# Running the long convolution among the steps of the recurrence, with each of its products split into two of 64 columns

## The chip, the cores and the metric

The kernel is one program on one core of a Trainium2 chip. The metric is device microseconds (us) of one execution, smaller is better. The kernel before takes 4325.55 us (median of 3 runs, 4324.6 to 4327.83).

## The reference

The model has two blocks. The part that matters here lies in its second block, in a layer whose input is projected, in one dense product, to the inputs of two branches. One branch is a recurrence over tokens, the other a long convolution; a dense output layer takes both results.

```python
def wkv_scan(s0, r, decay, k, v, kk, b, reverse, emit):
    def step(s, inp):
        r_t, w_t, k_t, v_t, kk_t, b_t = inp
        sa = jnp.einsum('bhij,bhj->bhi', s, kk_t)
        s = s * w_t[:, :, None, :] - sa[..., None] * b_t[:, :, None, :] + v_t[..., None] * k_t[:, :, None, :]
        y = jnp.einsum('bhij,bhj->bhi', s, r_t) if emit else None
        return s, y
    ...

def fft_long_conv(z, kern, skip):
    L = z.shape[1]
    zf = jnp.fft.rfft(z.astype(jnp.float32), n=2 * L, axis=1)
    kf = jnp.fft.rfft(kern, n=2 * L, axis=0)
    y = jnp.fft.irfft(zf * kf[None], n=2 * L, axis=1)[:, :L]
    return (y + z * skip).astype(z.dtype)

def hyena_operator(u, short_taps, kern, skip):
    v, x1, x2 = split_cols(centred_conv3(u, short_taps), (HY_WIDTH, HY_WIDTH, HY_WIDTH))
    z = v
    for o, gate in enumerate((x1, x2)):
        z = gate * fft_long_conv(z, kern[:, o], skip[o])
    return z
```

The recurrence runs for 8 heads of 64 channels and in two directions, first over 256 context tokens, then over 1024 latent tokens, where it also emits y. A readout normalises the sum of both directions' y for each head. The convolution is of order 2 over 512 channels and 1024 tokens.

## The kernel before, in words

Inside this layer the work comes in four stages, one after another.

1. **The dense input layer** (`rec_dense`). Its tasks are interleaved with the preparation of features (`rwkv_features`), among them `rwkv_inverse(who)`, which inverts small triangular matrices by doubling, with a product (L1660) and a subtraction (L1662) per step, and stores tables to DRAM (`d_T`). In this stage it runs for the head pairs 0 and 1 and for the context (`None`).
2. **The convolution** (`hyena`). `yH` holds the 512 channels as four tiles `ct` of 128 x 1024 tokens. For each order o and each half hh of 256 channels the tokens are transposed into `z` (L1268), go through a forward transform (L1281: a 128 x 128 block of the table `F` is stationary, 256 columns of z move), are combined and multiplied with the spectrum `K` on DVE (all through the helper `add`, L1271), giving `G`, and go back (L1338: a 128 x 128 block of G is stationary, 256 columns of the table `I` move). DVE then updates `yH`. The inverse products of one half are issued between the forward ones of the next.
3. **The recurrence** (`rwkv_chains`, `rwkv_scan`). Tokens are taken in 20 chunks of 64, heads in four pairs. A *chain* is one pair in one direction. Four chains run at once: pairs 0 and 1 in both directions for 20 steps, then pairs 2 and 3 for 20 more, 40 steps in all. Every four steps a chain has one load (`load`: be, LK, T and SV by DMA from SP's queue) and one preparation (`prep`: p2 at L1741, masked on DVE at L1746; pt at L1753, copied to `tm` by ACT at L1755; two more products L1763 and L1771, copied into AE and T). `LK` and `T` alternate between two buffers. A step (`steps`) has four parts, with a `yield` between them: pr (L1789) and its copy R; pu (L1799) and its copy `uv`, half on ACT and half on DVE; ps (L1806) and the new state (L1809, DVE: ps * PL + sp, where sp = SV * PL was made on POOL at L1795); py (L1815), copied or added into `yB`. The inverses of the pairs 2 and 3 run between the steps of the first 20 (`later`), on POOL, and the readouts of pairs 0 and 1 between the last 20 (`slow`).
4. **The dense output layer**, beside which the readouts of pairs 2 and 3 run.

A scheduler orders the instructions of each engine from the order in which the generators issue them and from when buffers come free, so each engine's order is near the code's, and not equal to it. The eight PSUM banks are shared out by name (`self.banks(name=count)`); a bank is taken anew when the last instruction that reads it is done. Bank and tile names in the orders below end in numbers that tell one use from another.

## Time and profile before

| what | us |
|---|---|
| median of 3 runs | 4325.55 |
| profiled execution | 4318.2 |
| its span | 4316.1 |
| end of the dense input layer | 1855 |
| convolution | 1855 to 2054 |
| recurrence | 2054 to 2454 |
| dense output layer | 2454 to 2546 |

The table's times come from the profiled execution, whose mean granted clock of PE is 0.939. The bounds of the stages are read from the instructions at their edges. In the profile, engines are PE (matrix products), PEld (its weight loads), DVE, ACT and POOL (elementwise) and SP (which issues most DMAs). A row of the groups gives line, engine, operation, result and operands with their shapes, count, then busy time, mean ns of one, then the idle time of the engine just ahead of them and what ended it. A row of the timeline gives start, length, engine, line, operation and how many instructions it stands for. A float32 product leaves two records.

### The profile page before, as it was taken

The page shows a single profiled execution, that of the slowest core. Times are in us where ns is not written, and L with a number is a line of the kernel's source. Part 1 is how long each engine was busy: PE and PEld are TensorE (multiplying, and loading weights), DVE is VectorE, ACT ScalarE, POOL GpSimd, SP SyncE. Part 2 cuts the span into 40 slices and gives each one's busy share as a digit, 9 for nine tenths or more (in the row PEclk, how much of TensorE's full clock was granted, in tenths as well). Part 3 has the DMA queues.
Part 4 walks back from the last instruction along what each step waited for, and adds up shares of the span by engine and source line. Part 5 has one row for each costly group of instructions (what it writes and reads, how often), then busy time and mean ns, then how long its engine had stood idle before and what let it go on. Part 6 is the DMA issues. An engine that isn't in the chain of part 4 may idle for free.

```text
span 4316.1 us, 65300 instructions
## 1 busy us (share of the span) xinstructions
PE 3887.0 (90%) x23789; PEld 3168.0 (73%) x23789; DVE 2779.1 (64%) x5935; ACT 1781.4 (41%) x3746; POOL 1357.6 (31%) x1570
## 2 busy tenths in 40 slices
PE   7989998899999988977686888999997897999999
PEld 4768886777787767766675766777876785888787
DVE  7842426788844767759565656599777768656532
ACT  6433415777735544411453423334336523333311
POOL 5422302333324432300564334122212116554200
PEclk8899998999999999988897999999998998999999
DMA  5444326421234544531543323233336351222422
GB/s 209 151 168 164 130 75 168 122 70 31 78 109 127 184 143 135 170 144 67 134 124 107 111 65 115 93 105 116 122 105 172 105 185 58 88 79 83 151 102 74
DMA packets 351338, 511.29 MB, mean 118 GB/s; under 512 B 149864, under 2 KB 226424, under 8 KB 348329
## 3 DMA queue, kind: packets, MB, share of 16 engines
q1 hardware_dynamic: 332200, 436.33, 32.1%
q0 software_dynamic: 14064, 53.48, 3.6%
q10 hardware_dynamic: 4752, 17.30, 1.3%
q8 instruction: 188, 3.08, 0.3%
q14 instruction: 134, 1.09, 0.1%
HBM read 343.69 MB, written 164.63 MB: 118 GB/s over the span
## 4 chain that ended last, share of the span: by engine, by line
PE 37%; DVE 7%; DMA 2%; ACT 2%; issue 1%; POOL 1%; SPq 1%; ACTq 0%; DVEq 0%; POOLq 0%
PE bank L285 18%; PE bank L2493 10%; PE bank L2393 2%; DMA SV<-d_V 1%; PE bank L1741 1%; PE bank L1789 1%; PE bank L724 1%; PE bank L1815 1%; PE bank L1753 1%; PE bank L685 1%; PE bank L246 0%; DVE d L2225 0%; DVE S L694 0%; DVE SV L1809 0%; DVE junk L2225 0%
## 5 line engine op out<-in xcount | busy, mean ns | idle before, releaser
L285 PE MATMUL bank<-hhi,whi 128*128 128x512 f32 (+1 forms) x1264 | 488.6, 387 | 13.1 <-ACT hhi L399 10.1
L285 PE MATMUL bank<-hlo,whi 128*128 128x512 f32 (+1 forms) x1264 | 485.0, 384 | 4.3 <-DVE hlo L400 2.1
L285 PE MATMUL bank<-hhi,wlo 128*128 128x512 f32 (+1 forms) x1264 | 482.6, 382 | 0.0
L267 ACT ACTIVATE whi<-wf 128x1024 fp32r<-128x1024 f32 (+3 forms) x202 | 193.5, 960 | 462.1 <-PE bank L285 393.0
L268 POOL TENSOR_TENSOR wlo<-wf,whi 128x1024 fp32r<-128x1024 f32 (+1 forms) x96 | 220.5, 2298 | 462.9 <-ACT whi L267 427.8
L285 PEld LDWEIGHTS bank<-hhi,whi 128*128 128x128 f32 x1264 | 243.8, 193 | 62.7 <-ACT hhi L399 10.9
L285 PEld LDWEIGHTS bank<-hlo,whi 128*128 128x128 f32 x1264 | 243.7, 193 | 54.5 <-DVE hlo L400 4.6
L285 PEld LDWEIGHTS bank<-hhi,wlo 128*128 128x128 f32 x1264 | 242.9, 192 | 46.7
L2493 PE MATMUL bank<-th,wh 128*128 128x512 f32 x616 | 247.3, 402 | 6.8 <-ACT th L2418 6.8
L2493 PE MATMUL bank<-th,wl 128*128 128x512 f32 x616 | 246.6, 400 | 0.0
L411 POOL CAST phi<-split 128x512 fp32r<-128x512 f32 (+1 forms) x104 | 62.7, 603 | 476.4 <-ACT split L410 381.0
L322 POOL TENSOR_TENSOR walo<-wa,wahi 128x512 fp32r<-128x512 f32 x96 | 137.0, 1441 | 238.4 <-ACT wahi L321 224.0
L285 PE MATMUL bank<-yT,whi 128*128 128x512 f32 (+1 forms) x600 | 190.6, 387 | 1.1 <-ACT ush L1393 0.5
L407 DVE TENSOR_TENSOR plo<-bank,phi 128x512 fp32r<-128x512 f32 (+2 forms) x260 | 166.5, 653 | 34.9 <-ACT phi L406 32.6
L406 ACT ACTIVATE phi<-bank 128x512 fp32r<-128x512 f32 (+2 forms) x260 | 143.5, 563 | 66.7 <-PE bank L724 25.4
L1795 POOL TENSOR_SCALAR sp<-SV,PL 64x64 f32<-64x64 f32 x304 | 135.9, 448 | 80.9 <-DVE SV L1809 59.4
L285 PE MATMUL bank<-yH,whi 128*128 128x512 f32 x376 | 151.4, 403 | 7.9 <-ACT ev_a L2156 4.4
L285 PE MATMUL bank<-yB,whi 128*128 128x512 f32 x376 | 150.6, 401 | 8.0 <-DVE yB L397 7.2
L285 PE MATMUL bank<-yH,wlo 128*128 128x512 f32 x376 | 150.4, 400 | 0.0
L268 DVE TENSOR_TENSOR wlo<-wf,whi 128x1024 fp32r<-128x1024 f32 (+2 forms) x106 | 117.6, 1112 | 50.8 <-ACT whi L267 50.6
L2493 PE MATMUL bank<-tl,wh 128*128 128x512 f32 x352 | 141.8, 403 | 6.4 <-DVE tl L2419 5.2
L2493 PEld LDWEIGHTS bank<-th,wh 128*128 128x128 f32 x616 | 117.7, 191 | 36.7 <-ACT th L2418 8.7
(632 smaller groups left out, 11275.9 us busy)
## 6 DMA issues: line engine op xcount, KB each, us to landing
wf<-in_w_in_dram SPq DMA_DIRECT2D x47, 512.0 KB, 3.5
wf<-in_w_ffn_in_dram SPq DMA_DIRECT2D x44, 512.0 KB, 3.4
d_rec<-r_rec SPq DMA_DIRECT2D x40, 512.0 KB, 3.6
wf<-in_rec_w_in_dram ACTq DMA_DIRECT2D x33, 512.0 KB, 3.9
wf<-in_attn_w_in_dram SPq DMA_DIRECT2D x26, 512.0 KB, 4.3
wa<-in_attn_ada_w_dram POOLq DMA_DIRECT2D x24, 512.0 KB, 4.0
wa<-in_rec_ada_w_dram POOLq DMA_DIRECT2D x24, 512.0 KB, 4.2
LK<-d_rec SPq DMA_DIRECT2D x64, 192.0 KB, 3.3
```

Of the source, the lines that this page charges most:

```text
L267: nc.scalar.activation(hi, wf, AF.Copy)
L268: self.wlo.tensor_tensor(lo, wf, hi, OP.subtract)
L285: self.mark = nc.tensor.matmul(ps[:, :n], w[:, k - k0, :], x(k, t0, n), start=(k == ks[0] and j == 0), stop=(k == ks[-1] and j == 2))
L322: nc.gpsimd.tensor_tensor(lo[:, k], w3[:, k], hi[:, k], OP.subtract)
L406: nc.scalar.activation(hi, src, AF.Copy)
L407: nc.vector.tensor_tensor(lo, src, hi, OP.subtract)
L411: nc.gpsimd.tensor_copy(hi, full)
L685: nc.tensor.matmul(bank[:, at:at + n], qs, kk[:, t0:t0 + n], start=(i == 0), stop=(i == 1))
L724: nc.tensor.matmul(o[:, c0:c0 + w], u["v"][:, kt, h, :], x[:, at:at + w], start=(kt == order[0] and j == 0), stop=(fin and j == 1))
L1795: nc.gpsimd.tensor_scalar(sp[half[h]], sv[half[h], h], pl[half[h]], None, OP.mult)
L2393: nc.tensor.matmul(ps, w[:, k, :], x[:, k, t0:t0 + n], start=(k == k0 and j == 0), stop=(k == k1 - 1 and j == 2))
L2493: self.mark = nc.tensor.matmul(ps, w[i][:, k, :], x[i][k], start=(k == 0 and j == 0), stop=(k == kh - 1 and j == 2))
```

## The change

The convolution becomes a generator (`hyena`) that runs between the steps of the recurrence (`scan_and_hyena`). It works by tiles of 128 channels, in eight rounds (o, ct), with halves of the buffers, and **every product is issued as two**, each with 64 stationary columns and 64 of the bank's partitions (`for h in (0, 64)`). Transposes become products with the identity. F and I are loaded at the start of the stage.

The recurrence runs **two chains at once instead of four**: both directions of one pair, one pair after another, 80 steps. Its banks are q=3 (pr, pu, ps), y=1, pt=1 for preparations, and X=2 for the convolution; readouts and inverses share one more. In a step, both halves of `uv` are copied by ACT; sp on POOL and the sum on DVE are gone: a product with the identity (L1792 of the kernel after) adds the state into the bank of ps, and ACT copies the bank into the next state with PL as scale. The second direction's y is copied by ACT and added on POOL. `uv`'s other half is loaded from DRAM where ACT copied it. A preparation has one bank in turn for its four products, and its masks come as two operations instead of four.

The inverse of pair 2 moves into the dense input layer; that of pair 3 runs between the first 20 steps. The readouts of pairs 0, 1 and 2 run between the steps of the next pair, and that of pair 3 beside the output layer.

```diff
-    def hyena(self, d_hy, d_sgh, yH):
...
-        self.banks(s=4, o=2, pt=2)
...
+    def hyena(self, pf, p, d_hy, d_sgh, yH):
...
+        for r in range(4):
+            nc.gpsimd.dma_start(yH[:, r], d_hy[r * 128:(r + 1) * 128, :])
+            self.load_r(F[:, r], A["dft_f1"][r])
+        for r in range(4):
+            self.load_r(I[:, r], A["dft_i1"][r])
+        yield
+        for o in range(2):
+            for ct in range(4):
+                G = []
+                yield from self.hyena_fwd(p, o, ct, F, yH, G)
+                yield from self.hyena_inv(p, o, ct, I, yH, G, d_hy, d_sgh)
...
-                    nc.tensor.transpose(ps[:, i * 128:(i + 1) * 128], zr[:, j // 2, (j % 2) * 128:(j % 2) * 128 + 128], self.ident)
...
+                for h in (0, 64):
+                    at = j % 2 * 128 + h
+                    nc.tensor.matmul(ps[h:h + 64, i * 128:(i + 1) * 128], zr[:, j // 2, at:at + 64], self.ident, start=True, stop=True)
...
-                        self.mark = nc.tensor.matmul(X[r][:, c], F[:, r, at:at + 128], z[:, r * 2 + k], start=(k == 0), stop=(k == 1))
+                        for h in (0, 64):
+                            at = k * 512 + c * 256 + f * 128 + h
+                            nc.tensor.matmul(X[r][h:h + 64, c], F[:, r, at:at + 64], z[:, r * 2 + k], start=(k == 0), stop=(k == 1))
...
-                            nc.tensor.matmul(ps[:, i, :], Gs[f][:, r, half, cc * 128:(cc + 1) * 128],
-                                             I[:, r, kt * 256:(kt + 1) * 256], start=(n == 0), stop=(n == 3))
+                        for h in (0, 64):
+                            nc.tensor.matmul(ps[h:h + 64, i, :], Gs[f][:, r, half, h:h + 64], I[:, r, kt * 256:(kt + 1) * 256],
+                                             start=(n == 0), stop=(n == 3))
...
+                                  (2, ("s", 3, 3), [("s", 2, g) for g in range(4)] + [("i", None)])):
...
-            later = [self.rwkv_inverse(p, pair, R, 1) for pair in (2, 3)]
-            self.banks(s=5, pt=2, o=1)
...
+            self.banks(q=3, y=1, X=2, pt=1, s=1)
+            self.share["o"] = self.share["s"]
+            self.rwkv_scan(p, R, yB, self.rwkv_inverse(p, 3, R, 1), self.hyena(q, q, R["hy"], R["sg"], yH))
...
+            for v in (x["S"], x["U"]):
+                for h in range(2):
+                    i = pair * 128 + h * 64
+                    nc.sync.dma_start(v[half[1 - h], :, h], R["V"][sg * 256:(sg + 1) * 256, i:i + 64].rearrange("(c s) i -> s c i", s=64))
...
-            p2 = [self.bank("pt", (128, 2, w, 64)) for _ in range(2)]
...
+            p2 = self.bank("pt", (128, 4, w, 64))
...
-                sp = T("sp", 4, 64)
-                for h in range(2):
-                    nc.gpsimd.tensor_scalar(sp[half[h]], sv[half[h], h], pl[half[h]], None, OP.mult)
...
-            nc.scalar.activation(uv[half[0], 0], pu[half[0]], AF.Copy)
-            nc.vector.tensor_copy(uv[half[1], 1], pu[half[1]])
...
+            for h in range(2):
+                nc.scalar.activation(uv[half[h], h], pu[half[h]], AF.Copy)
             if step < 19:
...
+                    nc.tensor.matmul(ps[half[h]], self.ident[:, half[h]], sv[:, h], start=True, stop=False)
+            yield
+            if step < 19:
+                for h in range(2):
+                    nc.tensor.matmul(ps[half[h]], tm[:, half[h]], uv[:, h], start=False, stop=True)
...
-                    nc.vector.scalar_tensor_tensor(s1[half[h], h], ps[half[h]], pl[half[h]], sp[half[h]], OP.mult, OP.add)
+                    nc.scalar.activation(s1[half[h], h], ps[half[h]], AF.Copy, scale=pl[half[h]])
...
+        for g in range(80):
...
+            gens = [steps(d, g) for d in range(2)]
...
             while gens or (preps and g % 4 == 3):
                 gens = [x for x in gens if next(x, 0) is None]
                 n += 1
+                turns += 1
                 if preps and g % 4 and next(preps[0], 0) is not None:
                     preps.pop(0)
...
+                if g < 20 and turns % 2:
+                    next(later, None)
+                if slow and n % 2 and next(slow[0], 0) is not None:
                     slow.pop(0)
+                if turns % 2:
+                    next(beside, None)
+        for _ in beside:
+            pass
```

The rows below are from the built orders of the two kernels: line, operation, result, operands, shape, and x with the number of like instructions in a row. Here is PE in the kernel before, in the middle of the convolution, where its transposes (L1268), inverse products (L1338) and forward products (L1281) stand.

```order
L1268 MATMUL bank4_4466_18930<-ident_1_66,yH_4394_18614 128x128 x4
L1268 MATMUL bank5_4469_18944<-ident_1_66,yH_4394_18614 128x128 x4
L1338 MATMUL bank6_4468_18939<-I_4404_18630,G_4453_18879 128x256 x2
L1338 MATMUL bank7_4471_18961<-I_4404_18630,G_4453_18879 128x256 x2
L1268 MATMUL bank4_4470_18954<-ident_1_66,yH_4394_18614 128x128 x4
L1268 MATMUL bank5_4472_18966<-ident_1_66,yH_4394_18614 128x128 x4
L1281 MATMUL bank0_4474_18978<-z_4465_18929,F_4395_18621 128x256 x4
```

And here is PE in the kernel after, in the convolution's second round: the forward products are now L1273, and the others belong to the recurrence (pr L1780, pu L1786, the identity L1792, ps L1796, py L1805) and to its preparations (L1763 and L1736, in bank6).

```order
L1273 MATMUL bank4_4619_20079<-z_4600_19958,F_4418_18767 64x128 x13
L1763 MATMUL bank6_4497_19330<-T11_4408_18734,AE1_4411_18740 64x32 x8
L1780 MATMUL bank1_4507_19379<-SV11_4445_18977,LK11_4407_18733 64x64 x2
L1786 MATMUL bank2_4511_19394<-R_4506_19377,T01_4403_18724 64x64 x2
L1792 MATMUL bank0_4512_19399<-SV01_4442_18965,ident_1_66 64x64 x2
L1273 MATMUL bank4_4619_20079<-z_4600_19958,F_4418_18767 64x128 x3
L1273 MATMUL bank5_4636_20166<-z_4600_19958,F_4418_18767 64x128 x11
L1786 MATMUL bank1_4513_19402<-R_4508_19382,T11_4408_18734 64x64 x2
L1792 MATMUL bank2_4514_19407<-SV11_4445_18977,ident_1_66 64x64 x2
L1796 MATMUL bank0_4512_19399<-UV01_4443_18966,tm01_4471_19137 64x64 x2
L1805 MATMUL bank3_4515_19426<-LK01_4402_18723,UV01_4443_18966 64x64 x2
L1736 MATMUL bank6_4525_19476<-LK00_4400_18719,eta0_4404_18727 64x128 x8
```

The convolution's products, which stood alone, now stand among those of two chains and of a preparation.

The second place is PE again, at a preparation in the recurrence. In the kernel before, its products (L1741, L1753, L1763, L1771) take the banks 5 and 6 in turn, and those of four chains (L1789 pr, L1799 pu) lie between.

```order
L1789 MATMUL bank2_5308_23286<-SV001_5120_22391,LK001_4545_19338 64x64 x2
L1753 MATMUL bank5_5299_23218<-ident_1_66,be_5243_23018 64x64 x16
L1763 MATMUL bank6_5305_23259<-T000_4544_19335 64x32 x8
L1789 MATMUL bank4_5314_23302<-SV101_5126_22411,LK101_4555_19358 64x64 x2
L1789 MATMUL bank0_5317_23310<-SV111_5129_22421,LK111_4560_19368 64x64 x2
L1799 MATMUL bank2_5321_23324<-R_5312_23297,T011_4551_19349 64x64 x2
L1771 MATMUL bank5_5307_23275<-T000_4544_19335,AE0_4563_19374 64x32 x8
L1741 MATMUL bank6_5324_23341<-LK010_4548_19344,eta01_4552_19352 64x128 x4
```

In the kernel after, at the end of its 14th block of four steps, the same products are L1755, L1763 and L1736.

```order
L1755 MATMUL bank6_5445_24530<-T01_4403_18724 64x32 x8
L1796 MATMUL bank1_5436_24463<-UV10_5346_23992,tm10_5398_24275 64x64 x2
L1780 MATMUL bank2_5446_24541<-SV00_5342_23979,LK00_4400_18719 64x64 x2
L1805 MATMUL bank3_5443_24522<-LK10_4405_18729,SV10_5345_23991 64x64 x2
L1805 MATMUL bank3_5443_24522<-LK10_4405_18729,UV10_5346_23992 64x64 x2
L1763 MATMUL bank6_5450_24551<-T01_4403_18724,AE0_4410_18739 64x32 x8
L1780 MATMUL bank0_5448_24546<-SV10_5345_23991,LK10_4405_18729 64x64 x2
L1786 MATMUL bank1_5453_24573<-R_5447_24544,T00_4401_18720 64x64 x2
L1792 MATMUL bank2_5454_24578<-SV00_5342_23979,ident_1_66 64x64 x2
L1805 MATMUL bank3_5457_24607<-LK00_4400_18719,SV00_5342_23979 64x64 x2
L1736 MATMUL bank6_5461_24623<-LK11_4407_18733,eta1_4409_18737 64x64 x8
```

All products of a preparation are in bank 6 now, and each waits there until the one before it has been read out.

The third place is DVE at the end of the dense input layer. In the kernel before, the evictions of its last tiles (L1416, 128x512) follow one another, and the next is the convolution's first operation (L1271).

```order
L1416 SCALAR_TENSOR_TENSOR osh_4381_18507<-ssh_4380_18506,bank2_4379_18481 128x512
L1416 SCALAR_TENSOR_TENSOR osh_4384_18537<-ssh_4383_18536,bank3_4382_18511 128x512
L1416 SCALAR_TENSOR_TENSOR osh_4390_18573<-ssh_4389_18572,bank0_4388_18547 128x512
L1416 SCALAR_TENSOR_TENSOR osh_4393_18603<-ssh_4392_18602,bank1_4391_18577 128x512
L1271 TENSOR_TENSOR W1_4415_18689<-W1_4415_18689,bank2_4413_18677 128x512 x2
```

In the kernel after, the same evictions are L1408, and the inverse of pair 2 (L1653 and L1655, products and subtractions of `ush` and `r_X`) ends among them.

```order
L1655 TENSOR_TENSOR r_X_4356_18314<-r_X_4356_18314,ush_4357_18315 128x30x2
L1408 SCALAR_TENSOR_TENSOR osh_4387_18629<-ssh_4386_18628,bank3_4385_18603 128x512
L1653 TENSOR_TENSOR ush_4357_18315<-r_X_4356_18314,r_U_4355_18313 128x31
L1655 TENSOR_TENSOR r_X_4356_18314<-r_X_4356_18314,ush_4357_18315 128x31
L1408 SCALAR_TENSOR_TENSOR osh_4393_18665<-ssh_4392_18664,bank0_4391_18639 128x512
L1408 SCALAR_TENSOR_TENSOR osh_4396_18695<-ssh_4395_18694,bank1_4394_18669 128x512
L1693 MEMSET T00_4401_18720 128x768
```

Its last product and subtraction stand ahead of the last two evictions, and the stage that follows begins with the clearing of T.

More of the change, by code (lines that the diff above doesn't have):

```diff
@@ L1775, in prep, with steps @@
             yield
-        def steps(ch, g):
-            pi, d = ch
-            pair, step = g // 20 * 2 + pi, g % 20
+        def steps(d, g):
+            pair, step = divmod(g, 20)
             c = chunk(d, step)
-            i, x = c % 4, loaded[ch, g // 4]
+            i, x = c % 4, loaded[d, g // 4]
             LK, tm, sv, uv = x["LK"], x["tm"][:, i], x["S"][:, i], x["U"][:, i]
@@ L1818, in steps @@
                     ysl = ysl[:, ::-1]
-                if (d == 0) == (c < 8):
-                    nc.scalar.activation(ysl, py, AF.Copy)
-                else:
-                    nc.vector.tensor_tensor(ysl, ysl, py, OP.add)
-        for ch in chains:
-            load(ch, 0)
-        for ch in chains:
-            for _ in prep(ch, 0):
-                pass
-        slow, preps = [], []
-        for g in range(40):
-            if g % 4 == 0 and g < 36:
-                for ch in chains:
-                    load(ch, g // 4 + 1)
-                preps = [prep(ch, g // 4 + 1) for ch in chains]
-            if g == 20:
-                assert not later
-                slow = [self.rwkv_readout(p, pair, R, yB) for pair in range(2)]
-            gens = [steps(ch, g) for ch in chains]
+                first = (d == 0) == (c < 8)
+                y = ysl if first else T("yt", 4, 64)
+                nc.scalar.activation(y, py, AF.Copy)
+                if not first:
+                    nc.gpsimd.tensor_tensor(ysl, ysl, y, OP.add)
+        for d in range(2):
+            load(d, 0)
+        next(beside)
+        for d in range(2):
+            for _ in prep(d, 0):
+                next(beside, None)
+        slow, preps = [], []
+        turns = 0
+        for g in range(80):
+            if g % 4 == 0 and g < 76:
+                for d in range(2):
+                    load(d, g // 4 + 1)
+                preps = [prep(d, g // 4 + 1) for d in range(2)]
+            if g % 20 == 0 and g:
+                assert next(later, 1) == 1 and not slow
+                slow = [self.rwkv_readout(p, g // 20 - 1, R, yB)]
+            gens = [steps(d, g) for d in range(2)]
             n = 0
```

219 lines of the change are left out of this document (92 added, 127 removed).

## The prediction

> **What bounds the kernel now.** I read the windows view first, cut at the edges of the two stages that the change merges and of the stretches inside the second one; its columns are the length, busy time and records of each engine, granted clock, DMA share and GB/s.
>
> ```profile
> core 0: us, PE busy (x) PEld busy (x) DVE busy (x) ACT busy (x) POOL busy (x), PEclk, DMA share, GB/s
> 1855.00:2054.00 199.00, 143.84 (x576) 118.45 (x576) 161.64 (x165) 26.96 (x41) 17.39 (x22) 0.81 0.30 110
> 2054.00:2086.00 32.00, 15.27 (x244) 14.43 (x245) 12.68 (x29) 8.97 (x26) 10.19 (x29) 0.59 0.64 169
> 2086.00:2270.00 184.00, 153.38 (x3472) 138.92 (x3470) 120.69 (x432) 93.67 (x379) 117.89 (x269) 0.93 0.49 124
> 2270.00:2308.00 38.00, 9.52 (x98) 8.39 (x96) 11.26 (x40) 4.43 (x9) 11.05 (x22) 0.56 0.29 75
> 2308.00:2454.00 146.00, 126.88 (x2439) 110.62 (x2439) 94.36 (x348) 68.56 (x286) 68.41 (x150) 0.92 0.31 85
> 1804.00:1855.00 51.00, 50.68 (x218) 40.38 (x216) 9.32 (x21) 10.39 (x14) 7.21 (x3) 1.00 0.33 90
> ```
>
> The convolution (first row) lasts 199 us. DVE is busy for 162 of them and ACT for 27: DVE is its bound, and PE waits for G. The recurrence (the next four rows) lasts 400 us. Each of its 40 steps moves four chains. In its last stretch 20 steps take 146 us, 7.3 each, or 29.2 us for a block of four steps, the length of one load and preparation. PE's 127 busy us are durations that overlap; by the distances of step 1 such a block needs 20.8 us of PE, so no engine is full.
>
> Between 2270 and 2308 nearly nothing runs. The chain of waits for that stretch names the reason:
>
> ```profile
> 2275.19 0.66 POOL ush L1660
> 2275.88 0.44 DVE r_X L1662
> ...
> 2296.66 2.58 DMA d_T<-r_U
> ```
>
> Pairs 2 and 3 start there, and their tables T come out of the inverse of pair 3, which still passes between POOL and DVE.
>
> **Step 1: what a product costs.** PE's records overlap, so I take distances between starts from the timeline of PE, not durations. A float32 product leaves two records.
>
> ```profile
> 2044.77 7.07 PE L1338 MATMUL bank<-I,G 128*128 128x256 f32 x32
> ...
> 2204.92 0.28 PE L1741 MATMUL bank<-LK,eta 128*64 128x128 f32 x1
> 2204.98 0.60 PE L1741 MATMUL bank<-LK,eta 128*64 128x128 f32 x7
> ...
> 2202.85 0.32 PE L1815 MATMUL bank<-LK,SV 128*64 128x64 f32 x4
> 2202.97 0.32 PE L1815 MATMUL bank<-LK,UV 128*64 128x64 f32 x4
> ...
> 2206.76 0.94 PE L1753 MATMUL bank<-ident,be 128*64 128x64 f32 x25 [0.21 <-DVE yB L1822]
> ...
> 2202.01 0.66 PE L1763 MATMUL bank<-T 128*64 128x32 f32 x16 [0.76 <-DVE LK L1746]
> ```
>
> A whole-width record with 256 columns moving comes every 7.07 / 32 = 0.22 us, so 128 columns would take 0.11. The half-width records of L1741, 128 columns moving, come every (0.60 - 0.28) / 6 = 0.053 us. Two halves in different columns therefore run side by side, and a pair costs what one whole product costs. The convolution becomes 1024 forward records x 0.053 = 55 us, 512 inverse records x 0.11 = 55 and 256 of its transposes, now products, x 0.053 = 14: 124 us of PE in all, as before except for the transposes.
>
> The Trainium skill ("TensorE: Matmul & The Clock Gate", Part 3: Packing small matmuls, The mechanism) speaks against this: a weight load overlaps running products only where its row group differs, and both halves use all rows. Here the trace disagrees, since half-width records with all 128 rows follow one another every 0.053 us.
>
> Four half records (two products) of the chain come every 0.12 us. A chain's step has 20 records now, and 24 with the added identity products, 0.72 us. A preparation has 16 records of 0.053, 32 of (0.94 - 0.22) / 24 = 0.03 and twice 16 of 0.03: 2.8 us. A block of four steps with two chains is thus 8 x 0.72 + 2 x 2.8 = 11.3 us of PE.
>
> **Step 2: what a block lasts without the convolution.** One round trip of a chain's step is read from the timeline.
>
> ```profile
> 2356.32 0.34 PE L1789 MATMUL bank<-SV,LK 128*64 128x64 f32 x4 [0.27 <-DVE SV L1809]
> ...
> 2356.76 0.22 ACT L1791 ACTIVATE R<-bank 128x64 f32<-128x64 f32 x1 [0.42 <-PE bank L1789]
> ...
> 2357.20 0.29 PE L1799 MATMUL bank<-R,T 128*64 128x64 f32 x4
> ...
> 2357.53 0.22 ACT L1800 ACTIVATE UV<-bank 64x64 f32<-64x64 f32 x1 [0.35 <-PE bank L1799]
> ```
>
> Start of pr to start of the next product is at most 0.88 us, handover 0.04 to 0.10. Three such trips make a step of about 2.5 us, with the second ACT copy of uv and of s1. Four make 10 us, so the step's latency does not set the block. The removed sp on POOL and the DVE sum were longer:
>
> ```profile
> L1795 POOL TENSOR_SCALAR sp<-SV,PL 64x64 f32<-64x64 f32 x304 | 135.9, 448 | 80.9 <-DVE SV L1809 59.4
> L1809 DVE SCALAR_TENSOR_TENSOR SV<-bank,PL,sp 64x64 f32<-64x64 f32 x304 | 85.5, 282 | 21.8 <-PE bank L1806 10.0 <-POOL sp L1795 2.4 <-POOL ush L1660 1.2
> L1746 DVE TENSOR_TENSOR LK<-bank,rmask 64x256 f32<-64x256 f32 x128 | 53.9, 421 | 18.4 <-PE bank L1741 16.2
> L1755 ACT ACTIVATE tm<-bank 128x512 f32<-128x512 f32 x40 | 23.7, 594 | 11.0 <-PE bank L1753 8.3 <-PE bank L1806 2.3
> L1766 ACT ACTIVATE AE<-bank 32x128 f32<-32x128 f32 x80 | 21.5, 269 | 12.1 <-PE bank L1763 9.3 <-PE bank L1789 0.5 <-PE bank L1806 0.2
> L1774 ACT ACTIVATE T<-bank 32x128 f32<-32x128 f32 x80 | 21.3, 266 | 11.7 <-PE bank L1771 10.4
> L1746 DVE TENSOR_TENSOR LK<-bank,rmask 64x128 f32<-64x128 f32 x32 | 9.2, 288 | 20.8 <-POOL eta L1737 15.1 <-PE bank L1741 5.2
> ```
>
> What is late next is the preparation: the change gives it one bank where it had two, so its four products and four evictions stand in one line. p2 is 0.85 + 0.28; two masks of 64x512, which no row shows, are 0.69 each by the slope from 288 to 421 ns; pt is 0.96 + 0.22; tm 0.59; ps 0.48 + 0.22; AE 2 x 0.27; ps 0.70; T 2 x 0.27. That is 6.6 us, and with eight handovers 7.3. Two in turn are 14.6 us. The first also waits for LK, whose buffer the block before has just left:
>
> ```profile
> LK<-d_rec SPq DMA_DIRECT2D x64, 192.0 KB, 3.3
> ```
>
> With two issues of 0.6 us that is about 4.4 us, and PE, which takes its queue in order, stands with it. I take 14.6 + 4.4 = **19 us**. The bounds are 14.6 (load hidden) and 29.2 (the pace of today's block, with twice the chains). It is nearer the first, because half the chains, and neither sp nor the sum, are left.
>
> **Step 3: with the convolution.** The order has its last product at the 52nd of 80 steps: 13 blocks hold it, 7 do not. It adds 124 / 13 = 9.5 us of PE to each, 20.8 in all. That is more than the line of preparations, so PE is the bound there. I keep the 4.4 us of standing and take **25.2 us**; the bounds are 20.8 and 29.2 + 9.5 = 38.7. DVE's 162 us of convolution over 13 blocks are 12.4 per block, with four masks of 0.69 15.2: below 25.
>
> **Step 4: the sum.** The start costs 32 us, as the row 2054:2086 has it: half the preparations, but the tables F come behind the fills on POOL. Three readouts, interleaved, I put at 4 us each (nothing, if gaps hide them, to about 10). 32 + 13 x 25.2 + 7 x 19 + 12 = 505 us, against 199 + 400 = 599: **94 us less**. The idle 38 us at 2270 go with that: the inverse of pair 3 now runs in the first steps and is wanted only at the 60th.
>
> The inverse of pair 2 moves under the last products of the dense layer:
>
> ```profile
> L1660 DVE TENSOR_TENSOR ush<-r_X,r_U 128x31 f32<-128x31 f32 (+15 forms) x31 | 17.4, 561 | 0.8
> L1662 DVE TENSOR_TENSOR r_X<-r_X,ush 128x31 f32<-128x31 f32 (+15 forms) x31 | 12.8, 412 | 0.8
> ```
>
> These are 30 us of DVE. From 1804 to 1855 DVE idles 42 of 51 us while PE is full: nothing; 30 us if that cover failed. Yet it ends just ahead of the layer's last evictions. SP's added loads of U (64 KB each, as SV) fill a queue that has a whole block for 18 transfers: nothing, up to a few us in the start.
>
> After the scan, one readout in place of two stands beside the output layer. The chain of waits from 2455 to 2550 gives their products L246, L1902 and L1874 together 15%:
>
> ```profile
> by line: PE bank L285 67.8%; PE bank L246 7.6%; ACT yhi L406 5.8%; PE bank L1902 5.5%; DMA wf<-in_rec_w_out_dram 3.5%; PE bank L1874 1.8%; ACT whi L267 1.6%; DVE ylo L407 1.5%; POOL wlo L268 1.0%; ACT bc_r L241 1.0%; issue 1.0%; ACT yB L189
> ```
>
> Half of 14 us is 7. In all 101 us less: the profiled execution's 4318.2 us (span 4316.1) become 4217, and on the scale of the median of the runs, 4325.55, the time is **4225 us**.
>
> **Rivals.** *PE never waits.* Gaps are filled so well that a block costs 20.8 and 14.6 us, and start and readouts 35: 408 us, 198 less with the output layer, 4128. For it: the order puts convolution products between almost all of the chain's. Against: none of today's stretches keeps PE's records close together (3472 in 184 us).
>
> *The line of preparations, lengthened by DVE's queue* (the slower side). The masks wait behind the convolution's operations on DVE, tm and the chain's copies behind those on ACT, and pt, in PE's order, holds up both chains.
>
> ```profile
> L1271 DVE TENSOR_TENSOR Y<-Y,T 128x1024 f32<-128x1024 f32 x16 | 18.9, 1225 | 0.0
> L1328 ACT ACTIVATE yH<-yH,cols 128x1024 f32<-128x1024 f32 x8 | 9.1, 1142 | 0.0
> ```
>
> One of the first kind ahead of each of the four masks is 4.9 us, and a few of the second make it 8. A block of 33 us with the convolution and 21 without gives 13 x 33 + 7 x 21 + 44 = 620, 14 more than today with the output layer: 4340. It decides from a mean block of (599 + 7 - 44) / 20 = 28 us. For it: one bank, and an in-order PE. Against: DVE is free for 40% of a 25 us block.
>
> *The halves do not run side by side* beside other work. Each forward record costs 0.11 and each inverse one 0.22: 124 us more of PE, 34.7 us per block, 13 x 34.7 + 133 + 44 = 628 and 22 more: 4348. Against it: L1741. It is what the rule of the Trainium skill on row groups (step 1) would bring.
>
> That the change does not do what it says is excluded by the order, in which the convolution's products stand among the chain's.
>
> **How the numbers follow.** My forecast has 0.76 (alone 4150 to 4310), PE never waiting 0.10, the line of preparations 0.09, the serial halves 0.05. The range 4130 to 4325 leaves out the slower two and the edges, some 2 in 10. A measurement of this kernel tells 0.2%, 8.7 us, from no change. Faster by more than that: nearly all of the forecast, the first rival and the mild half of the second, 0.85. Within: 0.05. Slower: 0.10.
>
> **What will show it.** The forward products should start 0.053 us apart, the inverse ones 0.11; twice that is the serial halves. The steps from the 53rd on should take 19 us per four, the earlier ones 25; 28 or more on average is the line of preparations. PE's idle before p2 should name the DMA of LK, and before pt the masks. The idle stretch at the change of pairs should be gone, and the dense layer should end where it did. I am wrong if a step's own latency (2.5 us) grows behind ACT, which now carries six of its operations per chain.

## The result, and the profile after

The changed kernel takes **4249.61 us** (median of 4 runs, 4244.72 to 4260.47) against 4326.28 beside it: 76.7 us less, a ratio of 0.9826 with a 95% interval of 0.9807 to 0.9846. Forecast were 4225 us, 101 less. Its profiled execution took 4251.05 us (span 4249.3, clock 0.951), 67 less than the one of before.

In what follows *the stage* is the time from the end of the dense layer's last eviction to the first product of the output layer, read from the timelines. It was 604.2 us (1856.0 to 2460.2) and is 540.7 (1859.9 to 2400.6). A *block* is four steps, from one first copy R to the next but three. The stage begins between 1856.9 and 1870.6 us in executions of kernels that are alike up to there, so kernels are compared by the stage as well as by the medians.

These are windows of the kernel after, at the edges of the start, of the blocks 1 and 2, 3 to 13, 14 to 20, and of what lies between the last step and the output layer; the columns are those of the prediction's windows.

```profile
1860.00:1886.00 26.00, 14.53 (x183) 13.90 (x182) 5.42 (x12) 3.02 (x6) 10.60 (x21) 0.67 0.95 305
1886.00:1971.00 85.00, 57.66 (x1024) 52.57 (x1026) 55.08 (x107) 36.18 (x127) 29.84 (x47) 0.83 0.50 127
1971.00:2267.00 296.00, 272.95 (x5237) 246.23 (x5234) 191.01 (x355) 183.36 (x689) 46.57 (x88) 0.97 0.48 131
2267.00:2391.00 124.00, 112.12 (x2245) 98.09 (x2245) 26.09 (x63) 97.94 (x393) 20.56 (x56) 0.96 0.39 103
2391.00:2401.00 10.00, 3.86 (x33) 3.36 (x30) 6.73 (x8) 8.90 (x15) 0.64 (x2) 0.76 0.65 242
```

The idle stretch at the change of pairs is gone: PE is busy for 385 of the 420 us from 1971 to 2391. The last product of the convolution is in block 13, as the order had it. What stands out is the second of the five rows. The first two blocks take 85 us, where eleven later ones with the convolution take 296, 26.9 each, and the seven without it 124, 17.7 each (the last of these, which is read only to its last R and has no preparation beside it, 10.8). The forecast had 32 for the start, 25.2, 19, and 12 for the readouts:

| part | forecast | measured | difference |
|---|---|---|---|
| start | 32 | 26.5 | -5.5 |
| blocks 1 and 2 | 50.4 | 84.8 | +34 |
| blocks 3 to 13, with two readouts | 277 + 8 | 296.1 | +11 |
| blocks 14 to 20, with one readout, and the end | 133 + 4 | 133.3 | -4 |
| stage | 505 | 540.7 | +36 |

PE's timeline gives the spacing of the two kinds of products; x is the number of records in a row.

```profile
1885.99 1.97 PE L1273 MATMUL bank<-z,F 128*64 128x128 f32 x32
1930.61 2.91 PE L1329 MATMUL bank<-I,G 128*64 128x256 f32 x24
```

With the last record's own length taken off, that is (1.97 - 0.23) / 31 = 0.056 us and (2.91 - 0.38) / 23 = 0.110: the forecast's 0.053 and 0.11.

Where the first block lost its time stands in PE's waits from 1886 to 1939 (total, times, longest), and in the timelines of DVE and SP.

```profile
PE bank L1780 <- DVE LK L1740: 7.8, 1, 7.8
PE bank L1747 <- DVE LK L1740: 6.8, 1, 6.8
```

```profile
1894.67 1.23 DVE L1258 TENSOR_TENSOR Y<-Z,K 128x1024 f32<-128x1024 f32 x1 [7.50 <-DMA K<-d_spec]
...
1900.66 0.88 DVE L1740 TENSOR_TENSOR LK<-bank,emask 64x256 f32<-64x256 f32 x2
...
1910.40 0.19 DVE L1655 TENSOR_TENSOR r_X<-r_X,ush 128x31 f32<-128x31 f32 x1 [6.00 <-POOL ush L1653]
```

```profile
1889.40 0.62 SPq L1262 DMA_DIRECT2D K<-d_spec  x1
```

SP issues the load of K at 1889.4, DVE waits 7.5 us for it with the mask (L1740) queued behind, and PE waits for the mask. Later a subtraction of pair 3's inverse (L1655) waits at the head of DVE's queue.

### The profile page after: what moved, and what is told of

Its sections match the earlier page's. It is cut to its first block, busy times and chain, and to the rows that moved or that the text cites. A ratio compares the mean times of both kernels' runs of the same rounds, so it can differ in the third digit from the quotient of the medians.

```text
span 4249.3 us, 68780 instructions
## 1 busy us (share of the span) xinstructions
PE 3885.8 (91%) x25613; PEld 3182.5 (75%) x25613; DVE 2678.9 (63%) x5484; ACT 1896.1 (45%) x4210; POOL 1245.1 (29%) x1299
## 5 line engine op out<-in xcount | busy, mean ns | idle before, releaser
L407 DVE TENSOR_TENSOR plo<-bank,phi 128x512 fp32r<-128x512 f32 (+2 forms) x260 | 166.5, 653 | 35.8 <-ACT phi L406 33.4
L698 ACT ACTIVATE P<-S,mx 128x768 f32<-128x768 f32 (+7 forms) x144 | 117.4, 816 | 63.6 <-DVE mx L694 56.9
```

Of the source, the lines that this page charges most:

```text
L407: nc.vector.tensor_tensor(lo, src, hi, OP.subtract)
L698: nc.scalar.activation(P[:, :at], S[:, :at], AF.Exp, bias=m[:, i:i + 1], scale=-1.0, accum_out=st["rs"][:, bi, u["h"]:u["h"] + 1])
```

## The experiments

Each is the changed kernel with one edit, but for spread_k_early, which joins two of them, and inverse_later, which has the edit of k_early beside its own. The stage is read from each one's trace. A ratio is to the kernel before as it ran beside that kernel, with medians of 4321.7 to 4329.2 us, so small differences go by the ratios and the stage, not by the medians alone.

| kernel | median us | ratio to before (95%) | stage us |
|---|---|---|---|
| before | 4326.28 | | 604.2 |
| after | 4249.61 | 0.9826 (0.9807 to 0.9846) | 540.7 |
| full_width | 4266.15 | 0.9859 (0.9843 to 0.9876) | 557.6 |
| half_runs | 4285.69 | 0.9895 (0.9880 to 0.9910) | 560.8 |
| no_conv | 4152.17 | 0.9588 (0.9566 to 0.9610) | 437.0 |
| conv_first | 4406.70 | 1.0175 (1.0160 to 1.0190) | 693.1 |
| spread | 4257.58 | 0.9849 (0.9835 to 0.9864) | 537.8 |
| k_early | 4254.76 | 0.9838 (0.9821 to 0.9854) | 536.4 |
| spread_k_early | 4261.83 | 0.9864 (0.9846 to 0.9882) | 543.7 |
| two_prep_banks | 4271.77 | 0.9873 (0.9852 to 0.9895) | 555.4 |
| dve_late | 4261.44 | 0.9862 (0.9843 to 0.9880) | 547.9 |
| dve_all | 4298.09 | 0.9941 (0.9928 to 0.9954) | 572.7 |
| stores_off_sp | 4254.41 | 0.9840 (0.9823 to 0.9857) | 542.3 |
| inverse_later | 4246.39 | 0.9817 (0.9797 to 0.9838) | 530.4 |

**full_width: what the halves cost.**

```diff
-                        for h in (0, 64):
-                            at = k * 512 + c * 256 + f * 128 + h
-                            nc.tensor.matmul(X[r][h:h + 64, c], F[:, r, at:at + 64], z[:, r * 2 + k], start=(k == 0), stop=(k == 1))
+                        at = k * 512 + c * 256 + f * 128
+                        nc.tensor.matmul(X[r][:, c], F[:, r, at:at + 128], z[:, r * 2 + k], start=(k == 0), stop=(k == 1))
...
```

> The changed kernel with the convolution's transposes, forward and inverse products issued as one of 128 columns instead of two of 64; all else, the interleaving too, stays. Theory (two halves run side by side and cost what one whole product costs): the forward records come 0.11 us apart instead of 0.057, the inverse ones 0.22 instead of 0.110, half as many of each; the two stages take the same 541 us within 13, and the time is 4250 within 13. Rival 1 (whole-width products do not mix well with the chains' 64-column ones: each change of width drains the array, some 8 changes in each of 50 steps at 0.1 us): 40 us more, about 4290. Rival 2 (a half costs more than half a whole): 40 us less or better, 4210 or below.

PE's timeline of this kernel, with the transposes' products (L1254), and then those of the changed kernel (L1255):

```profile
2012.97 3.54 PE L1254 MATMUL bank<-ident,yH 128*128 128x128 f32 x14
...
2112.72 1.95 PE L1271 MATMUL bank<-z,F 128*128 128x128 f32 x16
...
2150.17 2.86 PE L1326 MATMUL bank<-I,G 128*128 128x256 f32 x12
```

```profile
1982.83 1.71 PE L1255 MATMUL bank<-ident,yH 128*64 128x128 f32 x24
```

The spacing is (1.95 - 0.27) / 15 = 0.112 and (2.86 - 0.38) / 11 = 0.225: inside a run of forward or inverse products two halves cost what one whole costs. In the transposes they cost less: a whole record comes every (3.54 - 0.40) / 13 = 0.24 us, a half every (1.71 - 0.28) / 23 = 0.062, so 128 whole records take some 15 us longer than 256 halves.

The stage rose by 17 us and the time by 14 to 17 (by the ratios and by the medians), beyond the 13 allowed. By the distances between neighbouring records from 1880 to 2260, a whole-width record came 0.155 us after one of the chains, where a half came after 0.05 to 0.07, and a chain's record 0.21 to 0.29 after a whole one (0.11 to 0.22 of it the whole one's own), where 0.06 to 0.11 follow a half. Some 80 runs of convolution products have such a seam at each end: 16 us at 0.1 each. Rival 1 had the kind of the loss and the price of a seam, and too many seams; the transposes are a second loss, which the expectation does not have. Together they are some 31 us of PE for 17 us of time, and how the 17 divide between them was not tried.

**half_runs: who runs beside whom.**

```diff
-                for c in range(2):
-                    for k in range(2):
-                        for h in (0, 64):
+                for h in (0, 64):
+                    for c in range(2):
+                        for k in range(2):
...
```

> The changed kernel with the loop over the two column halves moved outside: four products (eight records) of one half, then four of the other; the same products otherwise, the transposes as they were. Theory (records of one half follow one another at the whole-width pace of 0.11 and 0.22 us, and only records of different halves run side by side; PE bounds the blocks that hold the convolution): 16 records take 14 slots instead of 8, so a forward record costs 0.096 us instead of 0.057 and an inverse one 0.19 instead of 0.110, 84 us more of PE in all; the time is 4300 to 4334. Rival 1 (the halves do not matter, a 64-column record costs 0.057 by itself): spacing and time as in the changed kernel, 4250 within 13. Rival 2 (the spacing doubles, but PE has room, since something else bounds the block): 4270 or less.

PE's timeline:

```profile
2106.94 0.38 PE L1273 MATMUL bank<-z,F 128*64 128x128 f32 x2
...
2107.28 0.87 PE L1273 MATMUL bank<-z,F 128*64 128x128 f32 x8
```

The first row has two records 0.38 - 0.27 = 0.11 us apart, the second has eight (0.87 - 0.27) / 7 = 0.086 apart. Records of one half follow one another at the whole-width pace; rival 1 is out. By the distances between neighbouring records the mean spacing was 0.073 and 0.150 us (0.059 and 0.114 in the changed kernel), less than the 0.096 and 0.19 expected: between the lone records of a run there were stretches in which both halves' records alternated. That is (0.073 - 0.059) x 1024 + (0.150 - 0.114) x 512 = 33 us more of PE. The stage of the profiled execution rose by 20 us and the time by 30 to 36 (by the ratios and by the medians): more than half of what PE takes longer is paid, which is against rival 2. At 4286 us the time lies below the 4300 of the theory and above the 4270 of that rival.

**no_conv and conv_first: the parts by themselves.**

```diff
-            self.rwkv_scan(p, R, yB, self.rwkv_inverse(p, 3, R, 1), self.hyena(q, q, R["hy"], R["sg"], yH))
+            self.rwkv_scan(p, R, yB, self.rwkv_inverse(p, 3, R, 1), self.no_hyena(q, R["hy"], yH))
```

> The changed kernel without the convolution: yH is only loaded, and no transform, spectrum product or inverse is computed. Theory (a block of four steps without the convolution costs 17.6 us, as the last seven blocks of the changed kernel do, whatever the pair): start 26, 20 blocks x 17.6 = 352 and 10 at the end: 388 us against 541, the time is 4097 within 20. Rival 1 (the preparation's one bank, or the inverse of pair 3, makes the early blocks as slow as they are, 27 us each): about 4210. Rival 2 (the late blocks are slow for their readouts, a bare block takes 13): about 4020.

```diff
-                nc.tensor.matmul(pr[half[h]], LK[:, h, 0, i], sv[:, h], start=True, stop=True)
+                mm = nc.tensor.matmul(pr[half[h]], LK[:, h, 0, i], sv[:, h], start=True, stop=True)
+                if g == 0 and h == 0:
+                    self.pace(mm, self.last)
...
+        for _ in beside:
+            pass
```

> The changed kernel with the first product of the recurrence made to wait for the last product of the convolution, so that the two run one after the other; the two-chain scan and the convolution by tiles of 128 with single buffers stay as they are. Theory (it is the overlap that pays): the scan's 388 us and a convolution of 200 to 240 us (in the kernel before 199 us, with halves of 256 channels and double buffers) stand one after the other: 47 to 87 us more, 4297 to 4337, about where the kernel before is. Rival (the gain is from the two-chain scan, which lost sp and the sum; the overlap only shifts work): 4250 within 13.

Windows of no_conv, at the start, blocks 1 and 2, the 18 others, and the end:

```profile
1865.00:1884.00 19.00, 4.22 (x57) 3.56 (x56) 3.62 (x6) 0.71 (x2) 7.95 (x17) 0.50 0.80 217
1884.00:1960.00 76.00, 48.68 (x760) 43.39 (x762) 17.57 (x42) 32.26 (x119) 20.38 (x43) 0.66 0.45 110
1960.00:2292.00 332.00, 301.17 (x6077) 265.50 (x6075) 75.67 (x187) 257.76 (x1034) 54.02 (x144) 0.96 0.45 116
2292.00:2302.00 10.00, 4.95 (x39) 4.32 (x33) 6.41 (x8) 8.83 (x17) 0.78 (x3) 0.64 0.70 254
```

The scan alone takes 437 us, not the 388 I expected, and 31 more than the four-chain scan of before (2054 to 2460, 406). So the two chains and the new state update won nothing by themselves. Beside them the convolution costs 541 - 437 = 104 us, against 199 in the kernel before: **the gain is the overlap**. Put first, the convolution takes 307 us (1862.4 to 2169.4), not the 200 to 240 I expected, and the kernel 4407, beyond the 4337 expected. Its operations wait for one another (PE waits 69 us for G there), which I put down to single buffers and tiles of 128, without a run of its own. 693 - 541 = 152 us are hidden in the changed kernel.

The first two blocks take 76 us even without the convolution, the 18 others 18.5 each. In conv_first, where the first loads and the inverse are done before the scan begins, they take 14.6 and 17.4. So some 44 us of the first two blocks come with the loads and the inverse, without any convolution. The inverse goes row by row, not by doubling: 31 products on POOL, and after each a subtraction on DVE. Timelines of DVE and POOL in no_conv show how the two meet:

```profile
1905.57 0.19 DVE L1661 TENSOR_TENSOR r_X<-r_X,ush 128x31 f32<-128x31 f32 x1 [15.96 <-POOL ush L1659]
...
1908.71 1.39 DVE L1746 TENSOR_TENSOR LK<-bank,emask 64x512 f32<-64x512 f32 x2
```

```profile
1904.32 0.85 POOL L1737 COPY eta<-be 64x256 f32<-64x256 f32 x2 [8.22 <-DMA be<-d_rec]
1905.31 0.23 POOL L1659 TENSOR_TENSOR ush<-r_X,r_U 128x31 f32<-128x31 f32 x1
```

The mask of block 1 stands on DVE behind a subtraction of pair 3's inverse, this waits for POOL, and there the product stands behind the copy of eta for block 2, which waits for its load be. Three queues in order make one chain of them.

**spread and k_early: when the convolution's work is done.** In spread the first product of each group waits for the latest pr; in k_early K has two buffers, loaded at a round's start.

```diff
+                            if c == 0 and k == 0 and h == 0:
+                                self.pace(mm, self.at_step)
...
-                if turns % 2:
+                if turns % 4:
                     next(beside, None)
```

> The changed kernel with the convolution's products tied to the steps of the recurrence, so that they spread over all 80 steps (32 to 72 forward products' worth per block of four steps, where the changed kernel has 48 to 102 in 13 blocks and none in the last seven). Theory (PE is full in the blocks that hold the convolution, 296 of 328 us, and has room in the seven others, where its records need 11.3 of 17.6 us): the seven blocks take a third of the products into their gaps, at less than the 0.8 us that one us of convolution costs in the full blocks (97 us for 124 of PE, from the run without it); 20 to 45 us less, 4205 to 4230. Rival 1 (what a product costs does not depend on where it stands, since gaps are the chains' own latency and every product lengthens it): 4250 within 13. Rival 2 (the convolution's own chain of transforms, single buffers, becomes late and its end holds up the output layer): 4265 or more.

```diff
+        Ks = [t("K", 4, 2, bufs=2) for f in range(2)]
+        for f in range(2):
+            nc.sync.dma_start(Ks[f].rearrange("p s c e -> p (s c) e"),
...
-            K = t("K", 4, 2)
...
+            K = Ks[f]
...
```

> The changed kernel with two buffers for the spectrum K, both loads issued at the start of a round (sgh takes z's buffer to make room); all else stays. Theory (the first block's 52.4 us come from K: SP issues its load behind 17 others at 1889.4, DVE waits 7.5 and 1.4 us for it and the masks of a preparation stand behind, PE waits 14.6 us for them): the first block takes about 38 us, and the time falls by 15, to 4235 within 8. Rival 1 (SP's queue makes be late as well: without the convolution the first two blocks take 42.1 and 33.8 us too): the first block stays above 42, at most 8 less, 4242 or more. Rival 2 (two loads of 512 KB ahead of the scan's first loads push those back): 4255 or more.

> Both of the edits above: the convolution spread over 80 steps and K with two buffers. If the two act on different blocks, their gains add up: 4190 to 4215. If the spread alone already takes the first block's convolution (64 products' worth instead of 102) out of the way of the masks, K adds nothing to it: as the spread alone, within 8.

Spreading moved the time from one place to another: the last seven blocks rose from 123 to 160 us, blocks 3 to 13 fell from 296 to 262, and the stage is 3 us shorter, which the medians don't tell from nothing. Rival 1: what a product costs does not depend on where it stands. In the changed kernel that is 26.9 - 18.9 (the same blocks of no_conv) = 8.0 us for 9.5 of PE, in each of the eleven blocks; in the last seven of spread 159.8 - 124.0 = 35.8 us for 43 of PE (320 x 0.056 + 192 x 0.110 + 64 x 0.062), 0.8 in both.

k_early left the first block at 55.5 us, but it does not say what an early K is worth. SP issued the first K behind the same loads as in the changed kernel, 27.1 us after the stage's begin instead of 29.5, and DVE still waited 5.4 us for it:

```profile
1896.26 1.77 SPq L1252 DMA_DIRECT2D K<-d_spec  x2
```

```profile
1900.91 1.23 DVE L1263 TENSOR_TENSOR Y<-Z,K 128x1024 f32<-128x1024 f32 x1 [5.39 <-DMA K<-d_spec]
```

Both edits together gave nothing either.

**two_prep_banks: the line of preparations.**

```diff
-            self.banks(q=3, y=1, X=2, pt=1, s=1)
-            self.share["o"] = self.share["s"]
+            self.banks(q=3, X=2, pt=2, s=1)
+            self.share["o"] = self.share["y"] = self.share["s"]
```

> The changed kernel with two banks in turn for a preparation's products instead of one; y shares the bank of readouts and inverses to make room. Theory (as forecast, the line of two preparations on one bank sets the late blocks): the blocks without convolution fall from 17.6 us to 15 or less, and all blocks by 2 on average: 4210 within 15. Rival 1 (those blocks are set by the steps' own products, which queue behind the preparation's on PE and ACT, whichever bank they take): 4250 within 13. Rival 2 (y behind a readout in the shared bank holds up PE's queue): 4265 or more.

The last four blocks, without convolution here, took 74.5 us together, against 68.7 in the changed kernel: a second bank did not shorten them, and the stage is 15 us longer, as rival 2 had it. That one bank does not set the pace is not shown by this: a readout ran beside three of the four blocks here, beside one of them in the changed kernel, and how much of the 15 is y in the shared bank was not tried. The first two blocks did fall, from 84.8 to 69.5 us; but the convolution ended only in block 15, and blocks 14 to 20 rose from 123 to 163.

**dve_late and dve_all: ACT's line of copies.**

```diff
-            for h in range(2):
-                nc.scalar.activation(uv[half[h], h], pu[half[h]], AF.Copy)
+            split = g >= 52
+            nc.scalar.activation(uv[half[0], 0], pu[half[0]], AF.Copy)
+            if split:
+                nc.vector.tensor_copy(uv[half[1], 1], pu[half[1]])
...
+                if split:
+                    nc.vector.tensor_scalar(s1[half[1], 1], ps[half[1]], pl[half[1]], None, OP.mult)
...
```

> The changed kernel with one of the two halves of uv and of the next state copied by DVE instead of ACT, in the steps from the 53rd on, where the convolution is done. Theory (a step waits for ACT: the copies of both chains stand in its one queue, R 2 x 0.22, uv 4 x 0.24, the state 4 x 0.33 and y, some 3.1 of the 4.4 us of a step, and ACT is busy for 97 of the last 123 us): 1.1 us per step go to DVE, which is busy for 26 of those 123 us; the late blocks fall from 17.6 to 13 to 15 us, 18 to 31 us less, 4219 to 4232. Rival (the steps wait for PE's queue, in which the preparations stand ahead, and ACT's copies are hidden): the late blocks stay within 1 us, 4250 within 10.

> The same split of the copies between ACT and DVE in all 80 steps. Theory (in the blocks with the convolution every engine's queue is mixed, and a chain's half on DVE stands behind operations of the convolution of up to 1.2 us, which takes back what ACT is relieved of): the late blocks fall as in the run before, the first thirteen stay within 2 us each: 4205 to 4250. Rival 1 (ACT's line of copies bounds all blocks): 13 x 3 us more than the late split alone saves, 4170 to 4190. Rival 2 (the convolution's operations ahead cost more than ACT's relief, some 0.6 us in each of 52 steps): slower than the late split by 25 or more, 4250 or more.

The window of dve_late over its late blocks (14 to 20), and the longest of DVE's waits there:

```profile
2278.00:2406.00 128.00, 112.57 (x2245) 100.92 (x2245) 51.98 (x169) 63.10 (x283) 20.57 (x56) 0.92 0.38 98
```

```profile
DVE UV L1790 <- ACT UV L1788: 41.2, 34, 6.5
```

ACT's busy time fell from 98 to 63 us and the blocks did not get shorter (128 against 123.4 us): ACT's load is not the bound. But DVE's half of uv began only when ACT's half was done, 34 times, so the two halves still stood in line, and the run does not say what two halves side by side would save. With all steps split, the convolution was done after eleven blocks, but these took 380 us, 34.5 each, and the stage is 32 us longer: the halves stand behind the convolution's operations on DVE, rival 2 of dve_all.

**stores_off_sp and inverse_later: the slow start.**

```diff
+        q = nc.gpsimd if pair in (2, 3) else nc.sync
...
-            nc.sync.dma_start(R["T"][h, 0:32, cs, 0:32].rearrange("s c t -> c s t"), U[i:i + 16])
+            q.dma_start(R["T"][h, 0:32, cs, 0:32].rearrange("s c t -> c s t"), U[i:i + 16])
...
```

> The changed kernel with the stores of the inverses of pairs 2 and 3, and the loads of pair 3's, issued from POOL's queue instead of SP's. Theory (the slow start is SP's queue: 12 stores of pair 2 hold it for 12.7 us just ahead of the recurrence's first loads, pair 3's loads and stores for 5.5 and 6.5 more ahead of be; without the convolution too the first two blocks take 42 and 34 us): the first preparation starts some 10 us sooner, the first two blocks fall from 85 to 70 or less: 4225 to 4240. Rival 1 (SP is late for its 0.6 us per issue of the two chains' own 36 first loads, whatever else stands there): 4250 within 10. Rival 2 (POOL, with F and I behind the stores and eta behind pair 3's, becomes late in SP's place): 4255 or more.

```diff
+                if pair == 3:
+                    self.pace(got, self.now)
...
-                if g < 20 and turns % 2:
+                if 8 <= g < 20:
                     next(later, None)
...
```

> The changed kernel with the inverse of pair 3 held back by eight steps (its loads wait for a product of the ninth step, and it ends before the 20th as before), and with the two early loads of K. Theory (the first two blocks take 85 us where later ones take 27 because of a chain of queues: DVE takes its operations in order, so a mask stands behind a subtraction of the inverse, which waits for POOL, where the product stands behind the copy of eta, which waits for be; and behind the spectrum product, which waits for K; without the convolution the same happened, 16 us in one piece): with both out of the way the first two blocks take 45 to 60 us and the time is 4215 to 4230. Rival 1 (the first loads themselves are late, since SP issues them 0.6 us apart and the DMA engines are full): the first two blocks stay at 75 or more, 4245 to 4260. Rival 2 (the wait moves with the inverse): the first two blocks fall below 65, and blocks 3 to 5 (75.7 us in the changed kernel) rise by as much: 4240 to 4255.

With the stores on POOL the first be was issued at 1856.9 instead of 1872.6, but yH's loads came late behind them (PE waited 9.4 us for yH). The first two blocks took 78.0 us, not the 70 expected, and the stage stayed. The time, 4254, is in the range of rival 1 and just under that of rival 2; the wait for yH is what rival 2 names.

With the inverse held back, the first two blocks fell from 84.8 to 69.7 us, and blocks 3 to 7 rose from 132.7 to 151.3. Against k_early, which shares the edit on K, they fell by 13 (82.6 to 69.7) and rose by 6 (145.2 to 151.3): about half of the wait moved with the inverse, which is nearest to rival 2, though the first two blocks are above its 65. K was as late as before here (29.3 us after the stage's begin, and DVE waited 6.8 for it). The stage is 10 us shorter, the medians (4246.4 and 4249.6) are not to be told apart. PE's waits of that kernel from 1855 to 1950 show what remains:

```profile
PE bank L1784 <- DVE LK L1744: 6.5, 1, 6.5
PE bank L1740 <- POOL eta L1735: 6.0, 1, 6.0
```

## Why the prediction was right, point by point

- **Step 1, the cost of a product: right.** The spacing is 0.056 and 0.110 us, and 0.062 for the transposes, and so the convolution takes 57 + 56 + 16 = 129 us of PE where 124 were forecast. The rule on row groups of the Trainium skill ("TensorE: Matmul & The Clock Gate", Part 3: Packing small matmuls, The mechanism) is not borne out: halves with all 128 rows run side by side, and half_runs shows that it is the columns that decide. Nor are the halves only neutral: their seams with the chains' products cost about 0.1 us less, and their transposes half as much.
- **Step 2, a block without the convolution: the number right (19 us, measured 17.7 and 18.5), in part by luck, the reason not borne out.** I had a step's latency at 2.5 us, "so the step's latency does not set the block", and took the preparations' one bank (the terms of a preparation there add up to 6.8, not 6.6, which changes little) and 4.4 us of standing for LK. But PE stood for LK 2.2 us in all seven blocks, as its waits from 2267 to 2390 have it:

```profile
PE bank L1736 <- DMA LK<-d_rec: 2.2, 3, 1.2
```

  That the one bank sets the pace, no run shows. Beside a preparation a step takes 4.4 us, with ACT and PE busy with one another's work between; in block 20, which has none, some 3.5. The luck: in no_conv, from the third block on, the first three blocks of a pair, among which the readout of the pair before runs, take 20.8 us on average, the others 16.7. A bare block is shorter than my 19, and if the rest is the readout's, it costs some 12 us where I had 4; the two errors offset. One step of one chain in the late blocks, from its pr to the next, ACT and PE in one timeline, shows what a step waits for:

```profile
2338.38 0.34 PE L1780 MATMUL bank<-SV,LK 128*64 128x64 f32 x4
...
2338.78 1.13 PE L1747 MATMUL bank<-ident,be 128*64 128x64 f32 x32
2338.78 0.23 ACT L1782 ACTIVATE R<-bank 128x64 f32<-128x64 f32 x1 [0.25 <-PE bank L1780]
...
2339.38 0.82 ACT L1890 ACTIVATE yB<-yB,cols 128x512 f32<-128x512 f32 x1
2339.73 0.29 PE L1786 MATMUL bank<-R,T 128*64 128x64 f32 x4
...
2340.22 0.60 ACT L1749 ACTIVATE tm<-bank 128x512 f32<-128x512 f32 x1
...
2340.71 0.45 ACT L1788 ACTIVATE UV<-bank 64x64 f32<-64x64 f32 x2
...
2342.09 0.55 ACT L1758 ACTIVATE AE<-bank 32x128 f32<-32x128 f32 x2
...
2342.66 0.64 ACT L1799 ACTIVATE SV<-bank,PL 64x64 f32<-64x64 f32 x2
...
2343.18 0.51 PE L1780 MATMUL bank<-SV,LK 128*64 128x64 f32 x4
```

  This step takes 4.8 us. pu waits on PE behind pt, uv on ACT behind a readout's copy and tm, the state behind AE: some 0.7, 0.7 and 1.0 us of queue beside the 2.5 of the trips. This is read from one step of the trace; the run that was to shorten it (dve_late) did not, so which of the queues counts most stays open. A step's latency that grows behind ACT is the sign that the prediction named for being wrong: it came, but four such steps are no more than the 19 us.
- **Step 3, a block with the convolution: 25.2 forecast (and 8 us for two readouts), 26.9 measured, readouts included; the rule not borne out.** I took the larger of two lines, PE's 20.8 us, and added 4.4. The runs show a sum instead: about 19 us of steps and 0.8 us for each us of PE that the convolution adds, wherever it is put (no_conv, spread; in half_runs 0.6 by the stage, 0.9 and more by the time). The two rules lie 2 us apart here. The last seven blocks of spread, with 6.1 us of convolution each, part them by what is added: the larger of the two lines would rise from 14.6 to 17.4, by 2.8 us, and the blocks rose from 17.7 to 22.8, by 5.1.
- **Step 4, the sum: where the 24 us were lost.** "The start costs 32 us" and 25.2 for every block is the term that was mis-sized: the first two blocks cost 85 us, not 50. The first loads and pair 3's inverse meet there in the in-order queues of SP, POOL and DVE: no_conv has the loss without the convolution, conv_first is free of it, and the two timelines show the chain. Which share each of the waits has stays open, since no run removed one alone. I had looked for a slow start only ahead of the first step. The stage lost 36 us against the forecast, the inverse of pair 2 another 3, and the output layer gave 3 back; on the profiled executions 67 us were won where 101 were forecast, 34 fewer. By the medians it is 24 fewer, and the 10 between are within what executions differ by. "The idle 38 us at 2270 go with that" holds for their place, but about as much came back at the front.
- **The inverse of pair 2, "nothing":** the dense layer ended 3.9 us later; its evictions stand 0.5 later at 1781 already, so 3.4 are the inverse's.
- **The output layer, 7 us:** at its first product the kernel is 59.6 us ahead of before, and at the 380th of the 384 products of this layer with yhi and ylo 69.9: 10.
- **The rivals:** PE never waiting fell with the 17.7 us blocks (14.6 needed), serial halves with the spacing. Of the line of preparations its lengthening by DVE's queue was real, in the first block above all (PE waited 14.6 us for masks there, and 4.5 from 1971 to 2267); the mean block was 25.2 us, below the 28 from which it would have decided.

## What to carry to other kernels

Work put beside a chain of dependent steps need not be free up to the busiest engine's limit: here it came on top of the chain, at 0.8 us for each us of PE, and still paid, because standing alone it took 199 us, and beside the chain 104. Judge the first iterations apart from the steady ones: first loads and one-time work shared queues there, and an operation that waited at the head of one held up what was ready behind it. Before an edit counts as a test, look whether it did what it was made for: the K of k_early came hardly sooner. Products of different column halves were interleaved here at no cost, where the halves alternate.

## What the runs showed of the hardware

Two 64-column records run side by side only in different halves (0.056 us apart against 0.11 in one half, 128 columns moving), and PE let a later half's records start between the earlier half's: in half_runs, where four products of one half stand ahead of four of the other, a record cost 0.073 on average, not the 0.096 of strict order. A change between 64 and 128 stationary columns cost about 0.1 us each way. A transpose's product with 128 stationary columns, read from yH, took 0.24 us a record, where two halves of 64 took 0.124.
